# One hybrid encoder layer on one core: elementwise work of the attention stage and of the turn to the channel mixer from GpSimd to VectorE and ScalarE, the turn in two passes, and the down projection's seven products chained in PSUM

## The chip, the core and the metric

The kernel runs on one core of a Trainium2 chip. The metric is the device time of one execution in microseconds; the time before is 1389.1 us, the median of three executions (1386.96 to 1390.07). TensorE (PE) does the matrix products, VectorE (DVE), ScalarE (ACT) and GpSimd (POOL) the elementwise work, and SyncE (SP) issues nearly all transfers.

## The reference, cut to what matters

One encoder layer on 1024 positions of width 1024. A combined input projection feeds gated linear attention (GLA, 4 heads) and differential attention (4 heads, each the difference of two softmax maps); the output projection of both joins the residual; a gated MLP with a depthwise convolution over positions follows, and a last RMSNorm.

```python
h = modulate(rms_norm(x, attn_norm_w), sh_a, sc_a)
q_g, k_g, v_g, r_g, lr_f, lr_b, q_d, k_d, v_d = split_columns(h @ w_in, IN_SIZES)
o_a = rms_norm(gla_forward(q_g, k_g, v_g) + gla_backward(q_g, k_g, v_g), gla_norm_w) * silu(r_g)
p = softmax(q_d @ k_d * scale + bias)            # two maps per head, blocks of 128 queries
o_b = rms_norm((p[0] - lam * p[1]) @ v_d, diff_norm_w) * 0.8
x = x + g_a * (concat(o_a, o_b) @ w_out)
h2 = modulate(rms_norm(x, ffn_norm_w), sh_f, sc_f)
u = conv3(h2 @ w_up)                             # 1024 x 5632
gate, val = split(u, 2)
x = x + g_f * ((silu(gate) * val) @ w_down)      # 2816 x 1024
return rms_norm(x, final_norm_w)
```

Everything is float32, to nearly float32 accuracy.

## The kernel before, in words

**Products.** Each operand of a large product is split into a high part, which ScalarE rounds to the format that TensorE takes (`split`, L369 and L370; `put_hi`, L390), and a low part, the difference, which VectorE or GpSimd takes (L371; `put_lo`, L394). `mm3` (L565 to L567) then runs three matmuls, high by high, low by high and high by low. The up and down projections run as seven products of half-size blocks in place of eight (Strassen's scheme in Winograd's form): sums of blocks are taken on VectorE ahead of a product, sums of results after it.

**Stages in order.** The start and the input projections, in an order written out by hand; from about 355 us the attention stage, in which the GLA heads, the differential attention (32 pairs of a head and a block of queries) and the output projection of the first 512 positions (`gen_wout(0)`) are interleaved; from about 690 us the last of the output projection of the second 512 positions (`gen_wout(1)`); the turn, in which the new x is normalised, transposed and made into the seven operands of the up projection; the up projection, 22 column blocks in pairs (`gen_up`); the down projection (`down_load`, `down_prep`, `down_mms`, `down_out`), and the last norm. Apart from the start the program's order is the order of priority of a list scheduler, which fixes each engine's queue beforehand by its own estimate of times. On the chip each engine takes its queue in order, so an instruction that waits holds all behind it.

**Attention.** `att_probs` makes scores, adds the bias and takes the row maximum on VectorE (L845) and the exponential on ScalarE (L850). `att_T` (L862) transposes the weights on TensorE in two halves, `aT`; one half is copied out by ScalarE (L871), the other by VectorE (L873). `att_out` multiplies by the values (L888) and, after each fourth block, scales by the norm on GpSimd (L898). The GLA heads make `gd` on GpSimd (L1022), and their `norm` (L1093) multiplies by the gate on GpSimd (L1099), rounds on ScalarE and takes the low part on GpSimd.

**The turn.** For each of four i, `gen_wout(1)` transposes two blocks (L380) and evacuates them on VectorE (`b12`, `b22`, L384), forms `t1` = b12 - b11 (L406), `t3` = b22 - b12 (L410), `t2` = t3 + b11 (L411) and `t4` = b21 - t2 (L412), and splits `t1`, `t3` and `b22` with GpSimd's low part, `t2` and `t4` with VectorE's. The first two column blocks of the up projection (`lead` in `strassen`) run beside it, step by step (L1594); the low parts of their weights are GpSimd's (L371).

**The down projection.** The products come in the order p1 p7 p6 p5 p4 p3 p2, each of six steps of up to 24 matmuls, in two sets of four PSUM banks in turn. Each result is taken out of its own bank, and `down_out` forms the sums with VectorE (L1557, L1561, L1562, L1568) and GpSimd (L1558); the gating (`x1_add`, L1538 and L1539) and the last norm's weight (L1565, L1571) are GpSimd's too except in p3 and p2. ScalarE squares the result (`half_sq`, L1545). Loads run three steps ahead (`AHEAD`).

**Buffers.** The pool `big` has 38 tiles of 128x1024, which all stages share; `half` has 5 of 128x512.

## Time and profile before

| | us |
|---|---|
| median of three executions | 1389.1 |
| the profiled execution | 1388.06 |
| its span, first to last instruction | 1386.4 |
| TensorE busy | 1302.7 |
| VectorE busy | 978.6 |
| ScalarE busy | 634.5 |
| GpSimd busy | 389.0 |

The mean granted clock of TensorE is 0.974 of full speed. A busy share is the union of the times of an engine's instructions; matmuls overlap in the records (each lasts 0.39 us and the next starts 0.23 us later), so a busy TensorE is not always one at its peak rate. A number in brackets at the end of a line of the timeline is the idle time of that engine just before the line, and what ended it. In the table of waits the time is summed over all waits of that kind.

### The profile page before, as it was taken

The page shows a single profiled execution, that of the slowest core. Times are in us where ns is not written, and L with a number is a line of the kernel's source. Part 1 is how long each engine was busy: PE and PEld are TensorE (multiplying, and loading weights), DVE is VectorE, ACT ScalarE, POOL GpSimd, SP SyncE. Part 2 cuts the span into 40 slices and gives each one's busy share as a digit, 9 for nine tenths or more (in the row PEclk, how much of TensorE's full clock was granted, in tenths as well). Part 3 has the DMA queues.
Part 4 walks back from the last instruction along what each step waited for, and adds up shares of the span by engine and source line. Part 5 has one row for each costly group of instructions (what it writes and reads, how often), then busy time and mean ns, then how long its engine had stood idle before and what let it go on. Part 6 is the DMA issues. An engine that isn't in the chain of part 4 may idle for free.

```text
span 1386.4 us, 17727 instructions
## 1 busy us (share of the span) xinstructions
PE 1302.7 (94%) x6244; PEld 1069.5 (77%) x6244; DVE 978.6 (71%) x1433; ACT 634.5 (46%) x1058; POOL 389.0 (28%) x284
## 2 busy tenths in 40 slices
...
GB/s 275 216 70 229 175 215 226 297 330 359 343 230 206 210 217 256 284 259 221 207 61 68 130 98 106 100 96 119 129 129 122 114 170 149 388 254 178 143 47 122
DMA packets 197873, 261.57 MB, mean 189 GB/s; under 512 B 13914, under 2 KB 122711, under 8 KB 197783
## 3 DMA queue, kind: packets, MB, share of 16 engines
...
q8 instruction: 49, 0.80, 0.2%
...
q10 hardware_dynamic: 372, 0.04, 0.0%
...
## 4 chain that ended last, share of the span: by engine, by line
PE 69%; DVE 12%; DMA 5%; issue 4%; ACT 3%; POOL 3%; SPq 2%; ACTq 0%; DVEq 0%; POOLq 0%
PE st_up_b L565 4%; PE st_up_b L566 4%; PE st_up_b L567 4%; PE s L842 3%; PE dp L566 3%; PE dp L565 3%; PE dp L567 3%; PE o L888 3%; PE st_up_c L566 3%; PE st_up_c L567 3%; PE st_up_c L565 3%; PE st_up_a L566 2%; PE st_up_a L565 2%; PE st_up_a L567 2%; PE wo_ps L567 2%
## 5 line engine op out<-in xcount | busy, mean ns | idle before, releaser
L371 POOL TENSOR_TENSOR wlo_up<-raw_up,whi_up 128x512 fp32r<-128x512 f32 x132 | 176.3, 1342 | 211.7 <-ACT whi_up L370 203.5
L370 ACT CAST whi_up<-raw_up 128x512 fp32r<-128x512 f32 x132 | 80.8, 618 | 110.9 <-PE st_up_b L566 61.1
L566 PE MATMUL dp<-wlo_dp,dp_hi 128*128 128x512 f32 x308 | 121.1, 393 | 8.3 <-DVE wlo_dp L371 8.3
L565 PE MATMUL dp<-whi_dp,dp_hi 128*128 128x512 f32 x308 | 119.9, 391 | 2.8 <-DVE dacc L1562 2.8
L567 PE MATMUL dp<-whi_dp,db_p 128*128 128x512 f32 x308 | 119.0, 391 | 0.0
L566 PE MATMUL st_up_b<-t_lo,whi_up 128*128 128x512 f32 x264 | 103.4, 392 | 4.4 <-DVE t_lo L394 4.4
L565 PE MATMUL st_up_b<-t_hi,whi_up 128*128 128x512 f32 x264 | 103.6, 393 | 3.8 <-ACT t_hi L390 2.7
L567 PE MATMUL st_up_b<-t_hi,wlo_up 128*128 128x512 f32 x264 | 102.8, 390 | 0.0
L850 ACT ACTIVATE p<-p,mx 128x1024 f32<-128x1024 f32 x64 | 73.5, 1149 | 50.1 <-DVE mx L845 49.8
L845 DVE CUSTOM_DVE_ANT_0 p<-s,bias 128x1024 f32<-128x1024 f32 x64 | 77.3, 1217 | 14.9 <-PE s L842 12.9
L1432 ACT ACTIVATE cv<-u,cw 128x1024 f32<-128x1024 f32 x44 | 53.2, 1210 | 61.0 <-DVE u L433 61.0
L842 PE MATMUL s<-k,q 128*128 128x512 f32 x256 | 78.0, 427 | 2.4 <-DMA k<-k_d 1.5
L566 PEld LDWEIGHTS dp<-wlo_dp,dp_hi 128*128 128x128 f32 x308 | 58.1, 189 | 22.4 <-DVE wlo_dp L371 10.4
L371 DVE TENSOR_TENSOR wlo_dp<-da_p,whi_dp 128x512 fp32r<-128x512 f32 x77 | 67.8, 896 | 8.1 <-ACT whi_dp L370 7.9
L888 PEld LDWEIGHTS o<-vd,aT 128*128 128x128 f32 x512 | 66.7, 199 | 6.8 <-issue 1.7
L371 DVE TENSOR_TENSOR db_p<-db_p,dp_hi 128x1024 fp32r<-128x1024 f32 (+1 forms) x42 | 59.6, 1425 | 16.9 <-ACT dp_hi L370 16.9
L565 PE MATMUL st_up_a<-b_hi,whi_up 128*128 128x512 f32 x176 | 68.9, 392 | 2.3 <-DVE b L384 1.3
L565 PEld LDWEIGHTS dp<-whi_dp,dp_hi 128*128 128x128 f32 x308 | 58.2, 189 | 15.3 <-DVE dacc L1562 3.2
L888 PE MATMUL o<-vd,aT 128*128 128x128 f32 x512 | 68.8, 284 | 0.9 <-ACT aT L871 0.9
L370 ACT CAST whi_dp<-da_p 128x512 fp32r<-128x512 f32 x77 | 46.4, 620 | 49.5 <-PE dp L567 37.5
L566 PE MATMUL st_up_a<-b_lo,whi_up 128*128 128x512 f32 x176 | 68.5, 389 | 0.0
L567 PEld LDWEIGHTS dp<-whi_dp,db_p 128*128 128x128 f32 x308 | 58.3, 189 | 12.1
...
## 6 DMA issues: line engine op xcount, KB each, us to landing
...
```

The costliest lines, as they stand in the source:

```text
L370: S.copy(out=dst_hi, in_=src)
L371: lo_eng.tensor_tensor(out=dst_lo, in0=src, in1=dst_hi.bitcast(F32), op=ALU.subtract)
L565: T.matmul(ps, wh, rh, start=first, stop=False, skip_group_check=more)
L566: T.matmul(ps, wh, rl, start=False, stop=False, skip_group_check=more)
L567: T.matmul(ps, wl, rh, start=False, stop=last, skip_group_check=more)
L842: T.matmul(s[:, tsl(n)], q4[:, 2 * m + sw, :], kd[h][m][:, tsl(n)], start=(sw == 0), stop=(sw == 1))
L845: V.tensor_tensor_reduce(out=t, in0=s, in1=bias, scale=1.0, scalar=3.0e38, op0=ALU.add, op1=ALU.min, accum_out=mx)
L850: S.activation(t, t, AF.Exp, scale=-1.0, bias=mx, accum_out=z[:, m:m + 1])
L888: T.matmul(o_ps, aT[:, k, :], vd[h // 2][k // 4][:, k % 4, psl(h % 2)], start=(k == 0), stop=(k == KT - 1))
L1432: S.activation(t, u[b], AF.Identity, scale=cw[:, 44 + ci:45 + ci], bias=cw[:, 132 + ci:133 + ci])
```

## The change

What it does:

- The turn leaves `gen_wout` and becomes `gen_turn`, and a string (`'turn'`) gives the order in which its steps (T, U, u), the steps of the first two column blocks (a letter and 0 or 1) and the rest of the output projection (L, W) are put into the program. A first pass (four T) makes `t1`, `b22` and `t3`, a second (two U, then u) `t2`, then the low parts of `t3` and `t4`. All low parts of the turn are VectorE's; the evacuation of `b22` becomes ScalarE's (`'tb'`). `t3` is kept in pairs of `big` in place of `half`.
- The first two column blocks take their products in the order 1 2 5 3 6 7 4, products 1 and 2, 5 and 3, and 6, 7 and 4 each chained in one bank; the low parts of all their weights are VectorE's (`'lv'`).
- Attention: both halves of `aT` are copied by ScalarE (`'aTs'`); `gd` (`'q3v'`), the scaling of `on` (`'onv'`), and the gate and the low part in GLA's `norm` (`'goe'`) become VectorE's. The list of output projection steps in each attention block (`'wo'`) is shifted.
- The down products come in the order p1 p2 p6 p7 p5 p4 p3. p2 adds to p1's bank, p7 and p4 to p6's, p3 to p5's, so that sums of results are formed in PSUM. GpSimd's `dacc` sums go; p2 gates on VectorE and adds on GpSimd; p4's last norm is one VectorE instruction of 128x1024 in place of the weight on GpSimd. `a12` is loaded twice, and the x of the first four tiles comes at step 3 in place of 27, that of the others at 21 in place of 22.

```diff
-    KN = {... 'wo': [3, 2, 2, 2, 2, 2, 1, 1, 2, 4, 3, 3, 3, 2, 3, 3], ... 'x01': (3, 4), ...}
+    KN = {... 'wo': [3, 2, 2, 2, 2, 2, 2, 2, 2, 3, 3, 3, 3, 2, 3, 3], ... 'x01': (3, 3), ...
+          'dord': 'p1 p2 p6 p7 p5 p4 p3', 'aTs': '01', 'ons': 0, 'goe': 'VV', 'q3v': 1, 'onv': 1,
+          'turn': 'L p0 p1 W a0 a1 b0 b1 T T T T s0 s1 U U c0 c1 d0 d1 u', 'tb': 1,
+          'los': {'t1': 'VVVV', 'b22': 'VVVV', 't2': 'VVVV', 't3': 'VVVV', 't4': 'VVVV'}, 'lv': '1253674'}
...
-            return w_block(src, f"{name}{n}", G)
+            return w_block(src, f"{name}{n}", V if lead and str(n) in KN["lv"] else G)
...
+        if lead:
+            s1 = half(f"s1_{name}", F32, [P, TH], "sum")
+            c1 = half(f"c1_{name}", F32, [P, 4, P])
+            w, w2 = block(a11, 1), block(a12, 2)
+            add(c1, a21, a22)
+            sub(a21, a11, a21)
+            sub(a11, c1, a11)
+            sub(a12, a12, a11)
+            yield
+            A = mm_ps(f"st_{name}a")
+            into(A, w, "b11", True)
+            S.copy(out=s1, in_=A)
+            yield
+            into(A, w2, "b21", False)
+            out(0, 0, A, None)
+            yield
+            w = block(c1, 5)
+            yield
+            C = s_ps(f"st_{name}c")[:, tsl(0)]
+            into(C, w, "t1", True)
+            out(1, 1, C, s1)
+            yield
+            into(C, block(a12, 3), "b22", False)
+            out(0, 1, C, s1)
+            yield
+            Bk = mm_ps(f"st_{name}b")
+            into(Bk, block(a11, 6), "t2", True)
+            out(0, 1, Bk, dst(0, 1))
+            yield
+            into(Bk, block(a21, 7), "t3", False)
+            out(1, 1, Bk, dst(1, 1))
+            yield
+            into(Bk, block(a22, 4), "t4", False)
+            out(1, 0, Bk, s1)
...
-            if g == KN["aT"]:
+            if str(g) in KN["aTs"]:
...
-        G.tensor_tensor(out=on, in0=on, in1=ss.unsqueeze(2).to_broadcast([P, 4, P]), op=ALU.mult)
+            V.tensor_tensor(out=on, in0=on, in1=ss.unsqueeze(2).to_broadcast([P, 4, P]), op=ALU.mult)
...
-            G.tensor_tensor(out=o, in0=o, in1=r_t[:, tsl(th)], op=ALU.mult)
+            eg[KN["goe"][0]].tensor_tensor(out=o, in0=o, in1=r_t[:, tsl(th)], op=ALU.mult)
...
-            split(hi, lo, o, G)
+            split(hi, lo, o, eg[KN["goe"][1]])
...
+        for i in range(KT // 2):
+            if i % 2 == 0:
+                t3p[i // 2] = big(f"b12_{i}", F32, PAIR)
+            b12, b22, t1 = t3p[i // 2][:, i % 2, :], half(f"b22_{i}"), half(f"t1_{i}")
+            f32_block(xn_late, i, a_ff, sh_ff, b12, "h2n", "ao")
+            f32_block(xn_late, i + 4, a_ff, sh_ff, b22, "h2n", "ao", KN["tb"])
+            V.tensor_tensor(out=t1, in0=b12, in1=h2f[i // 2][:, i % 2, :], op=ALU.subtract)
+            put_hi(h2b, "t1", i, t1)
+            put_hi(h2b, "b22", i, b22)
+            V.tensor_tensor(out=b12, in0=b22, in1=b12, op=ALU.subtract)
+            put_lo(h2b, "t1", i, t1, eng("t1", i))
+            put_lo(h2b, "b22", i, b22, eng("b22", i))
+            yield
+        part = lambda i: [p[:, i % 2, :] for p in (t3p[i // 2], h2f[i // 2], h2f[2 + i // 2])]
+        for i in range(KT // 2):
+            t3, b11, b21 = part(i)
+            V.tensor_tensor(out=b11, in0=t3, in1=b11, op=ALU.add)
+            put_hi(h2b, "t2", i, b11)
+            V.tensor_tensor(out=b21, in0=b21, in1=b11, op=ALU.subtract)
+            put_lo(h2b, "t2", i, b11, eng("t2", i))
+            if i % 2:
+                yield
+        for n, k in (("t3", 0), ("t4", 2)):
+            for i in range(KT // 2):
+                put_of(n, i, part(i)[k])
...
+    LOADS = {"p1": ("a11",), "p2": ("a12", "a21"), "p6": ("a22",), "p7": (), "p5": ("a21", "a22"), "p4": (), "p3": ("a12",)}
+    BANK = {"p1": ("A", True), "p2": ("A", False), "p6": ("B", True), "p7": ("B", False), "p4": ("B", False),
+            "p5": ("C", True), "p3": ("C", False)}
...
+            mm3(ps_of[t], bh[:, i, psl(t)], bl[:, i, psl(t)], *ws[i], new and u == 0, u == NU - 1, not new)
...
+        elif p == "p2":
+            x1_add(t, 0, ps, half(f"dt_{p}{t}"), (V, G))
+            half_sq(t, 0)
+        elif p == "p6":
+            tmp = half(f"dt_{p}{t}", tag="sum")
+            V.tensor_tensor(out=tmp, in0=ps, in1=s1, op=ALU.add)
+            s2_of[t] = tmp
         elif p == "p7":
+            V.tensor_tensor(out=kept(s3_of), in0=ps, in1=s1, op=ALU.add)
         elif p == "p5":
-            tmp = half(f"dt_{p}{t}")
-            V.tensor_tensor(out=tmp, in0=ps, in1=acc2[t], op=ALU.add)
-            V.tensor_tensor(out=acc1[t], in0=ps, in1=acc1[t], op=ALU.add)
+            tmp = s3_of[t // 2][:, t % 2, :]
+            V.tensor_tensor(out=tmp, in0=ps, in1=tmp, op=ALU.add)
             x1_add(4 + t, 1, tmp, tmp, (G, G))
             half_sq(4 + t, 1)
             G.tensor_tensor(out=x1[4 + t][:, TH:], in0=x1[4 + t][:, TH:], in1=fin_w[:, TH:], op=ALU.mult)
-            x1_add(4 + t, 0, acc1[t], acc1[t], (G, G))
+            x1_add(4 + t, 0, s2_of[t], s2_of[t], (G, G))
         elif p == "p4":
-            V.tensor_tensor(out=acc2[t], in0=ps, in1=acc2[t], op=ALU.add)
-            x1_add(t, 1, acc2[t], acc2[t], (G, G))
+            tmp = half(f"dt_{p}{t}")
+            V.tensor_tensor(out=tmp, in0=ps, in1=s1, op=ALU.add)
+            x1_add(t, 1, tmp, tmp, (G, G))
             half_sq(t, 1)
-            G.tensor_tensor(out=x1[t][:, TH:], in0=x1[t][:, TH:], in1=fin_w[:, TH:], op=ALU.mult)
-            p1 = p1_of[t // 2][:, t % 2, :]
-            x1_add(t, 0, p1, p1, (G, G))
+            finish(t, False)
...
+            V.scalar_tensor_tensor(out=o, in0=o, scalar=rs, in1=fin_w, op0=ALU.mult, op1=ALU.mult)
+            nc.sync.dma_start(out=out[0, psl(t), :], in_=o)
```

## Rows read from the trace of the kernel before

**Rows 1.** The first part of the page: busy us of each engine, its share of the span, and its instructions.

```profile
PE 1302.7 (94%) x6244; PEld 1069.5 (77%) x6244; DVE 978.6 (71%) x1433; ACT 634.5 (46%) x1058; POOL 389.0 (28%) x284
```

**Rows 2.** The view by windows of 20 us, some of them: the window, its length, busy us (and instructions) of PE, PEld, DVE, ACT and POOL, then the granted clock, the share of DMA and GB/s.

```profile
380.00:400.00 20.00, 17.71 (x105) 15.68 (x104) 14.96 (x31) 12.85 (x26) 1.89 (x1) 0.83 0.91 238
...
420.00:440.00 20.00, 15.77 (x91) 13.36 (x91) 11.18 (x19) 12.34 (x24) 5.92 (x6) 0.83 0.77 211
...
500.00:520.00 20.00, 18.51 (x118) 15.07 (x116) 12.28 (x21) 9.35 (x20) 3.67 (x3) 0.91 1.02 319
...
720.00:740.00 20.00, 11.45 (x36) 7.16 (x37) 19.93 (x19) 9.49 (x18) 14.70 (x10) 0.70 0.11 32
...
1200.00:1220.00 20.00, 20.00 (x90) 16.57 (x89) 19.14 (x22) 11.02 (x16) 0.00 (x0) 1.00 1.05 386
...
1320.00:1340.00 20.00, 16.07 (x69) 12.33 (x67) 18.17 (x13) 9.99 (x20) 20.00 (x11) 1.00 0.12 40
1340.00:1360.00 20.00, 18.96 (x76) 15.51 (x77) 15.73 (x26) 10.57 (x25) 2.13 (x2) 0.91 0.14 56
```

**Rows 3.** The same view with windows for whole stages: the turn, a part of the up projection, the down projection, the attention stage.

```profile
704.20:760.00 55.80, 41.77 (x169) 30.39 (x168) 46.63 (x53) 24.00 (x46) 34.04 (x23) 0.88 0.21 66
860.00:1080.00 220.00, 220.00 (x978) 182.31 (x977) 181.96 (x235) 98.02 (x137) 106.76 (x81) 1.00 0.39 118
1153.90:1378.00 224.10, 213.00 (x926) 173.99 (x924) 179.54 (x190) 100.86 (x169) 79.52 (x44) 0.99 0.52 184
...
355.00:690.00 335.00, 315.25 (x1948) 270.68 (x1947) 230.83 (x424) 170.50 (x353) 46.22 (x38) 0.96 0.80 241
```

**Rows 4.** The timeline of TensorE near the end, two matmuls 40 starts apart.

```profile
1355.03 0.39 PE L566 MATMUL dp<-wlo_dp,dp_hi 128*128 128x512 f32 x1
...
1364.10 0.39 PE L567 MATMUL dp<-whi_dp,db_p 128*128 128x512 f32 x1
```

**Rows 5.** VectorE's groups in the turn (704.2 to 748 us), by line and form: busy us, mean ns of one.

```profile
L394 DVE TENSOR_TENSOR t_lo<-h2f,t_hi 128x512 fp32r<-128x512 f32 x8 | 8.8, 1126 | 0.0
L384 DVE TENSOR_SCALAR b<-h_ps,a_ff,modc 128x512 f32<-128x512 f32 x8 | 6.2, 800 | 0.0
...
L1330 DVE TENSOR_SCALAR x<-x,rs_f 128x1024 f32<-128x1024 f32 x4 | 3.3, 838 | 3.1 <-ACT rs_f L366 3.1
L406 DVE TENSOR_TENSOR t<-b,h2f 128x512 f32<-128x512 f32 x4 | 2.7, 678 | 0.0
```

**Rows 6.** The timeline of VectorE and of GpSimd in the turn, and of SP's queue at its end.

```profile
720.84 1.77 DVE L412 TENSOR_TENSOR h2f<-h2f,h2f 128x512 f32<-128x512 f32 x1
...
720.33 1.74 POOL L394 TENSOR_TENSOR t_lo<-t,t_hi 128x512 fp32r<-128x512 f32 x1
...
737.12 29.25 SPq L1413 DMA_DIRECT2D raw_up<-in_w_up_dram  x11
```

**Rows 7.** GpSimd's groups in the attention stage (330 to 690 us), and the copies of `aT` in it (355 to 690 us) by VectorE and by ScalarE.

```profile
L371 POOL TENSOR_TENSOR go<-go,ohi 128x512 fp32r<-128x512 f32 x8 | 10.7, 1339 | 6.0 <-ACT ohi L370 5.3 <-DVE mx L845 0.7
L1099 POOL TENSOR_TENSOR go<-go,gr 128x512 f32<-128x512 f32 x8 | 10.2, 1276 | 62.0 <-DVE go L1098 56.6 <-PE aT_ps L869 5.4
...
L898 POOL TENSOR_TENSOR on<-on,oss 128x512 f32<-128x512 f32 x8 | 9.9, 1236 | 180.7 <-ACT oss L897 144.3 <-DVE mx L845 36.3
L1022 POOL TENSOR_TENSOR gd<-gq,dc_sh 128x1024 f32<-128x1024 f32 x4 | 7.6, 1906 | 36.5 <-DMA k_d<-qk_hi 21.9 <-DMA gq<-g_d 14.6
...
L873 DVE COPY aT<-aT_ps 128x512 f32<-128x512 f32 x32 | 22.0, 687 | 7.9 <-PE aT_ps L869 7.7
...
L871 ACT COPY aT<-aT_ps 128x512 f32<-128x512 f32 x32 | 18.6, 583 | 19.9 <-PE aT_ps L869 19.7
```

**Rows 8.** The timeline at two stops of TensorE in the attention stage: at 382 us (VectorE, TensorE) and at 431 us (ScalarE, TensorE), and TensorE at the two stops that follow.

```profile
380.34 1.70 DVE L1049 SCALAR_TENSOR_TENSOR gs<-gs,dc_sc,gs 128x128 f32<-128x128 f32 x1
...
382.36 0.65 PE L869 MATMUL aT_ps<-ident,p 128*128 128x128 f32 x4 [2.29 <-DVE on L889]
...
429.84 0.62 ACT L370 CAST ohi<-go 128x512 fp32r<-128x512 f32 x1 [2.17 <-POOL go L1099]
...
431.00 3.06 PE L1034 MATMUL u_ps<-gv,kn 64*128 64x128 f32 x16 [3.83 <-ACT kn L1029]
...
468.54 3.06 PE L1034 MATMUL u_ps<-gv,kn 64*128 64x128 f32 x16 [4.32 <-ACT kn L1029]
...
516.08 1.77 PE L842 MATMUL s<-k,q 128*128 128x512 f32 x4 [1.49 <-DMA k<-k_d]
```

**Rows 9.** VectorE's groups in the down projection, from 1160 to 1240 us and from 1276 to 1316 us.

```profile
L371 DVE TENSOR_TENSOR wlo_dp<-da_p,whi_dp 128x512 fp32r<-128x512 f32 x31 | 20.8, 684 | 4.2 <-ACT whi_dp L370 4.0
L371 DVE TENSOR_TENSOR db_p<-db_p,dp_hi 128x1024 fp32r<-128x1024 f32 x17 | 20.5, 1218 | 6.1 <-ACT dp_hi L370 6.1
...
L371 DVE TENSOR_TENSOR wlo_dp<-da_p,whi_dp 128x512 fp32r<-128x512 f32 x10 | 14.4, 1444 | 0.0
L371 DVE TENSOR_TENSOR db_p<-db_p,dp_hi 128x1024 fp32r<-128x1024 f32 x5 | 10.1, 2017 | 0.0
```

**Rows 10.** GpSimd's costliest group in the down projection (1236 to 1386 us); and what TensorE waited for over the whole run, two lines: us in total, times, longest.

```profile
L1538 POOL TENSOR_TENSOR dacc<-dacc,g_f 128x512 f32<-128x512 f32 x8 | 16.0, 2014 | 4.9 <-DVE dacc L1568 4.9
...
PE dp L566 <- DVE wlo_dp L371: 8.3, 5, 2.4
...
PE dp L565 <- DVE dacc L1562: 2.8, 1, 2.8
```

167 lines of the change are left out of this document (84 added, 83 removed).

## The prediction

> **What bounds the kernel now.** I read the busy shares first, then the windows, then the waits of the stages in which TensorE is not full. TensorE is busy for 1302.7 of 1386.4 us [rows 1], so nothing but TensorE's stops, and stretches at its lower clock level, can be won. In the up projection there are none: 220.00 of 220.00 us busy at a granted clock of 1.00, while VectorE has 182 of 220 [rows 3]. TensorE's rate at full clock is one 128x512 matmul per 0.227 us, from two matmuls 40 starts and 9.07 us apart [rows 4]. By that rate three stages lose time. The turn: 169 instructions in 55.8 us, of which 32 are transposes; 137 x 0.227 = 31.1 us, the transposes 6 us at most, so at least 18.7 us are lost [rows 3]. The down projection: 7 x 11 x 4 x 3 = 924 matmuls are 209.7 us in a stretch of 224.1, 14.4 lost [rows 3]. Attention: 335.0 - 315.3 = 19.7 us idle, and a mean clock of 0.96, some 13 us more [rows 3].
>
> One cause runs through all three. A VectorE instruction with two operands in SBUF takes 0.68 us where GpSimd is quiet and 1.77 where GpSimd works beside it [rows 5, 6]; in the down projection the same low parts go from 684 to 1444 ns and from 1218 to 2017 ns once GpSimd is loaded [rows 9]. In the turn VectorE is full (19.93 of 20 us) with such stretched instructions, TensorE has 11.45 of 20 and the clock falls to 0.70 in that window, after TensorE's stops [rows 2].
>
> **The turn: -12 us (-17 to -2).** GpSimd leaves it: its 19 low parts go to VectorE at 0.68 us each (the row of L406; 1.77 if GpSimd were still at work). VectorE's new work: first pass 4 x (0.80 for b12 + 4 x 0.68) = 14.1; second pass 12 x 0.68 = 8.2; low parts of t3 and t4 8 x 0.68 = 5.4; low parts of the weights of products 5 3 6 7 4 for two columns 6.8; ten result sums 6.8: together 41.3 us [rows 5]. The sums and weights of products 1 and 2 (12 x 0.68 = 8.2) come ahead of the last output projection part, and VectorE has room there. TensorE's work in the same stretch is 168 x 0.227 = 38.1 plus the transposes, 44.1. Counted from the last output projection matmul, VectorE can begin after the norm of x: 3.1 us idle and 3.3 of scaling in the rows of before, 6.4 [rows 5]; products 1 and 2 of both columns (48 matmuls, 10.9 us) cover that, and the chained order puts t1 and b22, which come first, under the next products. The first pass and two weights end at 6.4 + 15.5 = 21.9, the second, with two more weights, at about 31.5; TensorE is through with a, b, c, d and the transposes at 10.9 + 6 + 10.9 = 27.8: a stop of some 4 us. The last low part is done near 45, and 3 to 5 us of matmuls follow: 48 to 50 against 44.1. With the hand-overs to ScalarE I take a loss of 7 in place of 18.7: -12. The good end is a loss of 2 (-17). The bad end: if VectorE gets nothing back from the quiet GpSimd, it has 19 x 0.68 - 4 x 0.80 = 9.7 us more to do, which puts the loss at 17 (-2). One thing has no row: t3 in `big` tiles and the second pass hold more of the 38 tiles, so the loads for the third column, which SP's queue issues from 737.12 on, over 29 us [rows 6], start later against their use; I count that in the 7, up to 5 us.
>
> **Attention: -7 us (-17 to +5).** GpSimd gives up 38.4 us [rows 7]: `gd` 4 x 1.91, `on` 8 x 1.24, the gate and the low part 8 x 1.28 and 8 x 1.34. VectorE takes them at 4 x 1.22 (the 1218 ns row, [rows 9]) + 24 x 0.68 = 21.2 and hands 32 copies of 0.687 to ScalarE, 22.0: even. ScalarE gets 32 x 0.583 = 18.7 on 170.5 of 335, 56% [rows 3, 7]. What is won sits at the stops. At 380 us a 128x128 step that should be short took 1.70 beside `gd`, and TensorE stood for 2.29 behind VectorE [rows 8]: -2, and the stretch at half clock that follows (0.83 of 20 us, 3.4 us, [rows 2]): -3.4. At 431 and 468 ScalarE waits for GpSimd's gate (2.17), the copy `kn` stands behind it, and TensorE waits 3.83 and 4.32 [rows 8]; the gate on VectorE is 0.6 shorter, so -1.3 for both, because the chain of norm, gate, rounding and copy stays. At 516 a load is late behind a store of the low part [rows 8]: -1. Sum -7.7; +0.7 for the second half of `aT`, which now comes up to 0.58 later. Good end: all four stops (11.9) and 5 us of clock, -17. Bad end: a quarter of the 32 second halves uncovered, 4.7, and nothing won. The shifted list of output projection steps moves work within a stage that TensorE bounds; I cost it at nothing, with 2 us either way inside these ends.
>
> **The down projection: -4 us (-7 to +4).** After p5 and p4 GpSimd runs 40 instructions of some 1.95 us now (8 of them the group at 2014 ns, [rows 10]); after the change p5 keeps 20, p4 keeps 8, and p2 has 4. So the stretch after p5, where TensorE waits for `dacc` 2.8 us and part of the 8.3 for `wlo_dp` [rows 10], stays; that after p4 (1320 to 1346, TensorE 16.07 of 20, then clock 0.91, [rows 2]) loses 12 x 1.95 = 23 us of GpSimd beside VectorE. Of its 3.9 idle and 1.8 of clock I count two thirds: -4. Chaining adds waits: p2's first matmul into a bank waits for ScalarE's copy of p1 out of it, p7's and p4's for VectorE's sums. Behind those stand only the next matmuls, and a bank is asked for again three banks (2 us) later than its result is done, so they are free unless VectorE is late; 4 x 0.68 = 2.7 at worst. The second load of `a12` is 6 x 0.5 MB = 3.1 MB, 8 us at the 386 GB/s that the full queues give there [rows 2], with 4 MB of x now partly in the same stretch. SP issues them behind each other, ahead of the operands of the next steps; the lookahead of three steps (16 us) covers it, and if it does not, half of the 8 us shows: the +4.
>
> **Sum.** 1388.1 - 12 - 7 - 4 = 1365 for the profiled execution (its span of 1386.4 and 1.7 around it); the median, 1389.1, is 1 us above it. A difference under 0.2% (2.8 us) could not be told from no change.
>
> **The rivals.**
> As forecast, between 1352 and 1377: chance 0.58.
> VectorE becomes the bound. It is full in the turn already [rows 2], and gets 9.7 us more; if the end of GpSimd's work returns little of the stretching, the turn wins 2, attention, where its load is even, 3, the down projection 3: 1380 (1377 to 1385). For it: the full window; against it: 1.77 beside 0.68 in the same turn [rows 5, 6]. Chance 0.18. The Trainium skill bears on this one: its page "Perfetto Trace Analysis", under Optimizing Scalar/DVE Operations, advises to offload from a saturated VectorE to ScalarE or even GpSimd, the reverse of this edit, though it adds that the two share a read port, so that it might not help. By the first half the time would be the 1380 above, by the second the 1365; the rows named here speak for the second.
> The stops go with their half-clock stretches too, attention -17, turn -17, down -7: 1347. For it: each half-clock window in attention has a stop before or in it [rows 2, 8]; against it: the GLA chain stays long. Chance 0.13.
> The schedule made beforehand shifts and stops move elsewhere, so that nothing is won: 1388. Chance 0.04.
> Slower: ScalarE's queue in attention. Each block's second half of `aT` stands behind the first there; if TensorE has less than 0.58 us of other work between transposes and values, all 32 cost 18.7, and VectorE's low parts wait for ScalarE's rounding where GpSimd waited (5.3, [rows 7]), ahead of the row maxima: +24, against -16 from the other stages: 1396. It decides once those gaps are uncovered in over two thirds of the blocks. Against it: ScalarE is at 56%, and its copies wait 19.9 us for TensorE, not TensorE for them [rows 7]. Chance 0.07.
>
> **How the numbers follow.** Likeliest 1365. The range leaves out the slower and the unchanged case and half of the largest gain: 1347 to 1384. Faster 0.58 + 0.18 + 0.13 = 0.89, same 0.04, slower 0.07.
>
> **What would show it.** GpSimd with nothing between the last `on` and the third column, VectorE's instructions of the turn at 0.68 throughout, the clock at 1.00 there, and the turn's 169 instructions in about 44 us. In attention the low part of `go` on VectorE and stops at `kn` of 3 us or more still. In the down projection stops behind p5 but few after p4. Wrong would be: TensorE waiting for ScalarE's `aT`, stops on loads at 1190 to 1215, or a stop of many us at the third column.

## The result, and the profile after

The changed kernel takes 1372.3 us (median of 7 executions, 1368.7 to 1380.7) beside 1389.1 for the kernel before (7 executions on the same chip): a ratio of 0.9877, 95% interval 0.9854 to 0.9900. The forecast was 1365, between 1347 and 1384. The profiled execution took 1372.34 us, its span 1370.6; the span of before was 1386.4, so the two traces differ by 15.8 us. The busy line of the page after, against [rows 1]:

```profile
PE 1296.4 (95%) x6244; PEld 1065.0 (78%) x6244; DVE 957.6 (70%) x1447; ACT 649.3 (47%) x1086; POOL 287.5 (21%) x218
```

GpSimd gave up 101.5 us. VectorE, which took most of those instructions and handed 22 us of copies to ScalarE, is busy for 21 us less: its instructions got shorter. The windows of whole stages, columns as in [rows 3]: attention from the first transpose of the weights to the last matmul of the output projection, the turn, the same part of the up projection as before, the down projection.

```profile
363.68:702.08 338.40, 319.92 (x1956) 273.17 (x1955) 231.80 (x430) 189.73 (x390) 10.51 (x11) 0.95 0.77 233
702.20:760.00 57.80, 49.56 (x209) 37.85 (x208) 43.72 (x73) 28.49 (x55) 7.83 (x5) 0.94 0.23 73
860.00:1080.00 220.00, 220.00 (x978) 182.33 (x977) 182.77 (x232) 99.48 (x139) 105.69 (x80) 1.00 0.37 108
1146.40:1361.50 215.10, 211.09 (x925) 172.77 (x924) 165.79 (x185) 96.76 (x160) 55.69 (x32) 1.00 0.58 204
```

Each is read as before: what TensorE's matmuls would take at 0.227 us each is taken from the length. The turn: 209 instructions, 32 of them transposes (6 us): 177 x 0.227 + 6 = 46.2, a loss of 11.6 in place of 18.7 (the kernel before, over 57.80 us from 704.20, comes to 18.7 too). The down projection: 209.7 of 215.1, a loss of 5.4 in place of 14.4. The up projection's full part is unchanged. Where TensorE still stops, from its timeline:

```profile
424.14 1.73 PE L1051 MATMUL u_ps<-gv,kn 64*128 64x128 f32 x16 [1.43 <-ACT kn L1046]
...
461.43 3.09 PE L1051 MATMUL u_ps<-gv,kn 64*128 64x128 f32 x16 [3.65 <-ACT kn L1046]
...
509.69 1.17 PE L853 MATMUL s<-k,q 128*128 128x512 f32 x4 [2.28 <-DMA k<-k_d]
...
618.45 0.69 PE L380 MATMUL h_ps<-ident,x 128*128 128x128 f32 x2 [2.67 <-DVE x L1350]
...
745.90 0.47 PE L576 MATMUL st_up_b<-t_hi,whi_up 128*128 128x512 f32 x1 [2.12 <-DVE u L418]
...
802.66 0.50 PE L576 MATMUL st_up_a<-b_hi,whi_up 128*128 128x512 f32 x1 [2.90 <-DVE u L418]
...
1239.62 0.47 PE L576 MATMUL dp<-whi_dp,dp_hi 128*128 128x512 f32 x1 [2.52 <-DVE dt_p L1620]
```

Of [rows 8], the stop at 382 is gone, but two of 1.00 and 0.57 us stand before score matmuls at 384.82 and 386.99; those at `kn` are 1.43 and 3.65 in place of 3.83 and 4.32, and TensorE waits longer for the load of `k` (2.28 for 1.49). Three stops stand at a chained bank or a sum of results on VectorE: 745.90, 802.66 and 1239.62. Of the down projection's waits in [rows 10] only 0.7 us for `wlo_dp` is left.

In the turn VectorE's two-operand instructions, against [rows 5, 6] (its groups from 702.2 to 746 us, mean ns behind the busy time):

```profile
L371 DVE TENSOR_TENSOR wlo_up<-raw_up,whi_up 128x512 fp32r<-128x512 f32 x8 | 5.5, 699 | 3.1 <-PE h2n_ps L380 2.3 <-ACT whi_up L370 0.8
L394 DVE TENSOR_TENSOR t_lo<-h2f,t_hi 128x512 fp32r<-128x512 f32 x8 | 5.4, 702 | 0.0
...
L1382 DVE TENSOR_TENSOR t<-b,h2f 128x512 f32<-128x512 f32 x4 | 2.7, 686 | 0.0
```

From 720 to 740 us VectorE is full as before, but with 36 instructions in place of 19 [rows 2], and TensorE is busy for 16.09 us in place of 11.45, at a granted clock of 0.93 in place of 0.70:

```profile
720.00:740.00 20.00, 16.09 (x61) 11.07 (x60) 20.00 (x36) 11.49 (x21) 0.00 (x0) 0.93 0.05 14
```

Between the traces the last matmul of the output projection moved by 2.0 us (704.1 to 702.1; 1.3 of them lie ahead of the attention stage), the turn and the up projection shortened by 5.5 (449.9 to 444.4), and the down projection, first to last matmul, by 8.9 (223.7 to 214.8). The forecast was 7, 12 and 4.

### The profile page after: what moved, and what is told of

It is laid out like the page before. It is cut to its first block, busy times and chain, and to the rows that moved or that the text cites. A ratio compares the mean times of both kernels' runs of the same rounds, so it can differ in the third digit from the quotient of the medians.

```text
span 1370.6 us, 17665 instructions
## 1 busy us (share of the span) xinstructions
PE 1296.4 (95%) x6244; PEld 1065.0 (78%) x6244; DVE 957.6 (70%) x1447; ACT 649.3 (47%) x1086; POOL 287.5 (21%) x218
## 4 chain that ended last, share of the span: by engine, by line
PE 72%; DVE 11%; DMA 9%; issue 3%; ACT 2%; SPq 1%; POOL 1%; ACTq 0%; DVEq 0%; POOLq 0%
PE st_up_b L576 4%; PE st_up_b L577 4%; PE st_up_b L578 4%; PE s L853 3%; PE dp L576 3%; PE dp L577 3%; PE o L899 3%; PE dp L578 3%; PE st_up_a L576 3%; PE st_up_a L578 3%; PE st_up_a L577 3%; PE st_up_c L577 2%; PE st_up_c L578 2%; PE st_up_c L576 2%; PE pr_qk L576 2%
## 5 line engine op out<-in xcount | busy, mean ns | idle before, releaser
L371 POOL TENSOR_TENSOR wlo_up<-raw_up,whi_up 128x512 fp32r<-128x512 f32 x120 | 162.3, 1358 | 309.9 <-ACT whi_up L370 188.2
L578 PE MATMUL dp<-whi_dp,db_p 128*128 128x512 f32 x308 | 115.6, 389 | 0.0
L371 DVE TENSOR_TENSOR wlo_dp<-da_p,whi_dp 128x512 fp32r<-128x512 f32 x77 | 61.7, 823 | 20.3 <-ACT whi_dp L370 20.2
L576 PEld LDWEIGHTS dp<-whi_dp,dp_hi 128*128 128x128 f32 x308 | 57.8, 188 | 16.9 <-issue 2.9
L577 PEld LDWEIGHTS dp<-wlo_dp,dp_hi 128*128 128x128 f32 x308 | 57.8, 188 | 13.3 <-DVE wlo_dp L371 1.6
L578 PE MATMUL st_up_a<-b_hi,wlo_up 128*128 128x512 f32 x176 | 67.3, 390 | 0.0
L578 PEld LDWEIGHTS dp<-whi_dp,db_p 128*128 128x128 f32 x308 | 57.8, 188 | 11.9
```

The source lines that it names most:

```text
L371: lo_eng.tensor_tensor(out=dst_lo, in0=src, in1=dst_hi.bitcast(F32), op=ALU.subtract)
L576: T.matmul(ps, wh, rh, start=first, stop=False, skip_group_check=more)
L577: T.matmul(ps, wh, rl, start=False, stop=False, skip_group_check=more)
L578: T.matmul(ps, wl, rh, start=False, stop=last, skip_group_check=more)
```

## The experiments

The theory after the result had three parts. Theory 1: GpSimd was worth little in attention, because the stops at `kn` are made by the order of the queues. Theory 2: in the turn GpSimd's contention was what cost, and what is left is VectorE handing over results late. Theory 3: the down projection won so much because eight GpSimd instructions left the crowded stretch behind p5. Ratios are to the kernel before on the same chip; "us" is the ratio times 1389.1. The last three columns are lengths in one trace of each, from start to start: first `aT_ps` to last `wo_ps` matmul, from there to the first `dp`, first to last `dp`. "Span x clock" is the span times the mean granted clock, on the mean of a kernel's executions (before: the 71 beside the experiments): the span less what TensorE's lower clock level costs, if TensorE had work all that time. Its standard errors are 0.4 to 1.4.

| run | ratio (95%) | us | span x clock | attention | turn and up | down |
|---|---|---|---|---|---|---|
| before | 1 | 1389.1 | 1350.3 | 339.1 | 449.9 | 223.7 |
| changed | 0.9877 (0.9854, 0.9900) | 1372.0 | 1340.7 | 338.4 | 444.4 | 214.8 |
| changed, again | 0.9898 (0.9865, 0.9931) | 1374.9 | 1343.2 | 335.8 | 447.8 | 214.3 |
| attention as before | 0.9922 (0.9895, 0.9949) | 1378.3 | 1343.3 | 337.8 | 446.7 | 216.7 |
| down as before | 0.9930 (0.9909, 0.9951) | 1379.4 | 1346.8 | 337.8 | 442.8 | 221.6 |
| turn's low parts on GpSimd | 0.9942 (0.9921, 0.9963) | 1381.0 | 1344.9 | 334.5 | 450.1 | 215.6 |
| `kn` on VectorE | 0.9905 (0.9883, 0.9928) | 1375.9 | 1342.3 | 331.6 | 442.8 | 215.0 |
| `kn` ahead of the norm | 0.9923 (0.9895, 0.9951) | 1378.4 | 1342.8 | 332.3 | 442.8 | 216.5 |
| p5's gating held | 0.9963 (0.9942, 0.9984) | 1384.0 | 1346.3 | 336.0 | 444.3 | 225.7 |
| `aT` split | 0.9962 (0.9936, 0.9987) | 1383.8 | 1348.1 | 347.4 | 445.4 | 216.7 |
| attention's moves undone | 0.9944 (0.9926, 0.9963) | 1381.3 | 1347.8 | 342.8 | 444.9 | 214.2 |
| `gd` and `on` on GpSimd | 0.9906 (0.9878, 0.9933) | 1376.0 | 1345.5 | 336.3 | 442.2 | 215.6 |
| weights of 7 and 4 on GpSimd | 0.9867 (0.9844, 0.9890) | 1370.6 | 1341.8 | 336.6 | 444.2 | 213.8 |
| product 6 ahead of 3 | 0.9855 (0.9818, 0.9892) | 1369.0 | 1338.0 | 336.5 | 441.9 | 215.8 |

Executions of one kernel spread by about 0.5% to either side, so two ratios tell a difference apart only from some 0.4%. The trace of a stage tells more, but it spreads too: in the kernels whose edit does not touch it, attention lies between 334.5 and 338.4, turn and up between 442.2 and 447.8, down between 213.8 and 216.7.

**The changed kernel once more.**

> The changed kernel once more, unedited, on the chip and beside the same runs of the kernel before as the three edits that go with it. If the differences between executions are those of TensorE's clock alone (seven executions lie between 1368.7 us at a mean granted clock of 0.979 and 1380.7 at 0.972), span times mean clock is 1340 to 1342 us here too, the median is 1371 to 1376, and a second trace has the same stops at the same instructions (1.4 and 3.7 us at kn, 2.1 at the third chained bank of the turn, 2.5 at p7 in the down projection), with half-clock stretches in other places of the attention stage. If stops move as well, span times clock differs by more than 2 us.

A median of 1374.0 us, ratio 0.9898. The stops that were named stand at the same instructions with the same lengths: 1.43 and 3.65 at `kn`, 2.12 in the turn, 2.90 in the up projection, 2.53 at p7. Others differ: there is one of 1.06 us for the load of `q` at 432.60, and attention's idle time is 20.2 us for 18.5. The clock did not follow the stops alike; windows of 10 us, the granted clock is the third column from the end, first this kernel's first trace, then the second:

```profile
420.00:430.00 10.00, 7.91 (x44) 6.47 (x43) 6.63 (x11) 6.59 (x16) 0.00 (x0) 0.79 0.90 250
430.00:440.00 10.00, 10.00 (x71) 8.94 (x71) 7.81 (x15) 8.05 (x17) 0.20 (x1) 0.87 0.76 261
```

```profile
420.00:430.00 10.00, 7.91 (x58) 6.62 (x57) 6.94 (x12) 6.62 (x15) 0.00 (x0) 1.00 0.89 258
430.00:440.00 10.00, 8.88 (x69) 7.41 (x68) 7.92 (x15) 9.09 (x19) 0.20 (x1) 1.00 0.88 286
```

TensorE is busy for the same 7.91 us with the same stop of 1.43, once partly at the lower level, with 44 instructions, and once at full clock, with 58. The turn in the second trace, from the last output projection matmul, loses 57.8 - (184 x 0.227 + 6) = 10.0 us:

```profile
700.60:758.40 57.80, 50.53 (x216) 38.52 (x215) 45.20 (x74) 29.96 (x57) 8.26 (x6) 0.94 0.23 73
```

Span times mean clock is 1340.7 us on the mean of the first 7 executions (standard error 1.0) and 1343.2 of these 6 (1.4). So the expectation of 1340 to 1342 was missed by 1 us, and the two differ by the 2 us and more that I had named as a sign of stops that move, though hardly beyond these errors. I use span times clock below where a median says too little; the kernel before has 1349.9 to 1351.0.

**Attention alone put back.**

```diff
-    'wo': [3, 2, 2, 2, 2, 2, 2, 2, 2, 3, ...], 'aTs': '01', 'goe': 'VV', 'q3v': 1, 'onv': 1
+    'wo': [3, 2, 2, 2, 2, 2, 1, 1, 2, 4, ...], 'aTs': '0', 'goe': 'GG', 'q3v': 0, 'onv': 0
```

> The changed kernel with the attention stage alone put back as it was: one half of aT copied by VectorE, gd, the scaling of on, the gate and the low part in norm on GpSimd, and the old list of output projection steps. Theory 1 (the stops at kn come from ScalarE's own queue, in which the copy kn stands behind a rounding that waits for norm and gate; taking GpSimd out of it shortens that chain by about 1 us only): +2 us on 1372 (0 to +4), the last matmul of the output projection at 703 to 706 us in place of 702.1, stops of TensorE at kn of 3.5 to 4.5 us. Rival 1 (the predicted 7 us were won, and were lost again in the same stage through ScalarE's 32 more copies): also about +2, so this run sizes the part, and the run with the copies alone put back decides. Rival 2 (the attention stage owes its 2 us to nothing in these edits, only to the trace): 0, the last matmul at 702.

1378.3 us, 5 above the changed kernel (1373.5, the mean of its two rows), hardly told apart from it; by span times clock 1.4 us more (1343.3, against 1341.9 over the 13 executions of the changed kernel). The stage in the trace is 337.8, as the changed kernel's; the last matmul came at 702.06, not at the 703 to 706 that theory 1 expected. Its stops are those of [rows 8] again: 1.99, 3.84, 4.33 and 1.86 us. So attention brought some 1 to 5 us, hardly clear of the noise, and what by which edit this run can't say.

**`aT` split; all moves undone; two of them undone.** Three edits of the same four settings:

```diff
-    'aTs': '01'
+    'aTs': '0'
```

> The changed kernel with one edit in attention: the second half of aT is copied by VectorE again (32 copies of 0.69 us), ScalarE keeps the first. Theory 1 (GpSimd's work was worth little in attention, and ScalarE has room for the copies): 0, between -1 and +2 us, the stage unchanged within 2 us and only the wait for aT of 1.2 us at 626 us gone. Rival 1 (the moves off GpSimd won up to the 7 us forecast, and ScalarE's 32 more copies gave them back): -3 to -6 us, waits for ScalarE in the stage shorter. Rival 2 (VectorE is the tighter engine there): +3 and more, waits of TensorE for VectorE's row maxima or on.

```diff
-    'goe': 'VV', 'q3v': 1, 'onv': 1
+    'goe': 'GG', 'q3v': 0, 'onv': 0
```

> The changed kernel with ScalarE keeping both halves of aT and the old moves undone: gd, the scaling of on, the gate and the low part in norm go back to GpSimd, so that VectorE is rid of 21 us of work on both counts. After the run with half of aT put back on VectorE (6 to 8 us slower) there are two readings. Theory A (VectorE's load is what counts in attention; 22 us of copies were worth 6 to 8 us, so 21 us of other work are worth about as much): -3 to -7 us against the changed kernel's 1372 to 1374, VectorE busy about 207 us of the stage in place of 228. Theory B (GpSimd's slowness costs as much: its work stretches VectorE's beside it, and the gate on the norm chain takes 1.3 us in place of 0.69): 0 to +4, the stops at kn back at 3.8 and 4.3 us, as in the kernel before.

```diff
-    'q3v': 1, 'onv': 1
+    'q3v': 0, 'onv': 0
```

> The changed kernel with only gd and the scaling of on back on GpSimd (12 instructions, 10.5 us on VectorE); the gate and the low part of norm, which lie on the chain ahead of kn, stay on VectorE. Theory A (VectorE's load counts): -2 to -4 us, the stops at kn as in the changed kernel (1.4 and 3.7). Theory B (GpSimd stretches VectorE's work beside it): +1 to +3, with the 2 us stop of TensorE behind on at 382 us back, where gd runs beside the state's scan.

With the copies back on VectorE 1383.8 us, 10 slower; with the moves undone 1381.3, 8 slower; with `gd` and `on` alone on GpSimd 1376.0, not told apart by the ratio. The attention windows of the three, in this order:

```profile
369.09:716.51 347.42, 319.97 (x1956) 272.00 (x1955) 248.62 (x462) 172.29 (x358) 10.51 (x11) 0.95 0.75 227
```

```profile
369.73:712.54 342.81, 315.88 (x1956) 269.18 (x1955) 215.46 (x402) 189.77 (x390) 48.46 (x38) 0.97 0.76 230
```

```profile
364.10:700.36 336.26, 313.77 (x1957) 266.74 (x1956) 227.46 (x418) 188.92 (x390) 25.43 (x22) 0.97 0.76 235
```

TensorE idles for 27.5, 26.9 and 22.5 us (length less busy), against 18.5 and 20.2 in the two traces of the changed kernel. For `aT` split rival 2 holds by its price: VectorE, with 248.6 us of work for 231.8, is the tighter engine. The longest waits are not the ones that it named, though: 3.39 us for the load of `k`, 4.24 for the x that VectorE scales for the turn's first half. For the moves undone theory B holds in its sign, at twice its price: VectorE has 16 us less to do, and it is slower all the same. The stop at the second `kn` is 4.33 again, and at the end of the stage TensorE waits for GpSimd and for what comes behind it:

```profile
700.00 0.66 PE L924 MATMUL oT_ps<-ident,on 128*128 128x128 f32 x4 [1.21 <-POOL on L915]
701.44 0.50 PE L576 MATMUL wo_ps<-whi_wo,ok 128*128 128x512 f32 x1 [0.78 <-ACT ok L934]
```

These two, 1.45 us for VectorE at 696, 3.50 at 624 (2.67 in the changed kernel) and 1.7 more at `kn` make up most of what is lost. Putting back both halves (with the old list of steps) costs less than either alone: moves and copies are a swap, and each half needs the other. The third run splits the moves: `gd` and `on`, 4 instructions of 1.9 us and 8 of 1.2 on GpSimd [rows 7], make no difference that the ratio can tell, but by span times clock they cost 3.6 us (standard error 1.2) of the 5.9 that all moves cost, with 2 us and more of idle time beyond the changed kernel's. The 2 us stop behind `on` that theory B expected at 382 is not there (0.56 and 0.77 for `aT` are, at 383 and 385). The other 2 us, hardly told apart, are left for the gate and the low part, which stand ahead of `kn`: in this run the stops there are 0.90 and 3.65, with both back on GpSimd 2.48 and 4.33.

**The copy `kn` on VectorE, and ahead of the norm.**

```diff
-            S.copy(out=kn, in_=kps)
+            V.tensor_copy(out=kn, in_=kps)
```

> The changed kernel with one edit: the copy kn of the GLA heads (eight of them) out of PSUM is VectorE's in place of ScalarE's. Theory 1 (kn stands in ScalarE's queue behind a rounding that waits for the norm chain): the stops of TensorE at kn (1.43, 3.65 us) go or fall under 1 us, with part of the half-clock stretch behind each, total -3 to -7 us on 1372. Rival 1 (VectorE's queue holds kn as long, behind the row maxima and the gate): the stops stay at 1.5 to 4 us with VectorE as the engine named, total -1 to +2. Rival 2 (what stops there is TensorE's own order, the transposes of kn coming too late for a copy of 0.6 us to be hidden): the stops stay at 1.4 and more whoever copies, total 0.

```diff
             S.copy(out=kn, in_=kps)
+            if later:
+                later.pop()()
...
-        norm(1, *n1)
+        if h < 2:
+            later.append(lambda: norm(1, *n1))
+        else:
+            norm(1, *n1)
```

> The changed kernel with the second norm of GLA heads 0 and 1 put into the program behind the next head's first copy kn, so that kn no longer stands behind the norm chain in any queue; engines and work are the same. Theory 1 (the stops at kn are a matter of queue order: kn's transposes are done by 417.9 and 457.8 us, the copy is issued at 423.5 and 460.8, behind a rounding that waits for the gate): the two stops go from 1.4 and 3.7 to under 1.5 us together, total -2 to -6 us on 1372 with the half-clock stretches behind them. Rival (the delay comes back at the next reader: the norm's late low parts hold TensorE's output projection or the five half tiles): stops of 2 us and more at another instruction within 30 us, total -1 to +3.

1375.9 and 1378.4 us: neither is faster than the changed kernel, by span times clock either (1342.3 and 1342.8 for 1341.9). On VectorE the copy stands behind the same chain (timeline of TensorE, then of VectorE at 423 us):

```profile
425.45 1.68 PE L1051 MATMUL u_ps<-gv,kn 64*128 64x128 f32 x16 [2.29 <-ACT ohi L370]
...
460.88 1.82 PE L1051 MATMUL u_ps<-gv,kn 64*128 64x128 f32 x16 [3.16 <-ACT ohi L370]
```

```profile
423.27 0.75 DVE L1115 SCALAR_TENSOR_TENSOR go<-go,cols,gsq 128x512 f32<-128x512 f32 x1 [1.36 <-ACT gsq L1114]
424.06 0.69 DVE L1117 TENSOR_TENSOR go<-go,gr 128x512 f32<-128x512 f32 x1
424.67 0.68 DVE L1046 COPY kn<-kn_ps 128x512 f32<-128x512 f32 x1
```

`kn`'s transposes were through at 422.3; VectorE held the copy behind the norm and the gate until 424.67. The profile names ScalarE's rounding, but the copy's end, 425.35, lies 0.1 us before the matmul. That is rival 1. Put ahead of the norm, `kn` keeps TensorE for 0.39 us at most, but other stops of the same size are there in its place:

```profile
456.63 1.80 PE L853 MATMUL s<-k,q 128*128 128x512 f32 x4 [2.58 <-issue]
...
492.94 1.13 PE L1114 MATMUL ms<-gsq,inv_dv 128*128 128x512 f32 x2 [1.33 <-ACT gsq L1109]
```

TensorE's idle time in attention is 18.6 and 18.4 us in these two (331.64 less 313.00 busy, 332.34 less 313.98), inside the 17.9 to 20.3 of the seven traces that leave attention alone. Their stages are 4 us shorter in the trace because TensorE had a higher granted clock in that execution: 0.983 over the span, where the mean over all executions of the two is 0.979 and 0.976. So theory 1 is half right: the stops are a matter of queue order, but taking them away doesn't shorten the stage.

**The turn's low parts on GpSimd.**

```diff
-    'los': {'t1': 'VVVV', 'b22': 'VVVV', ..., 't3': 'VVVV', ...}, 'lv': '1253674'
+    'los': {'t1': 'GGGG', 'b22': 'GGGG', ..., 't3': 'GGGG', ...}, 'lv': ''
```

> The changed kernel in which the turn keeps its two passes and its order of products, but the low parts of t1, b22 and t3 and those of the first two columns' weights go back to GpSimd, as in the kernel before. Theory 2 (GpSimd's work beside VectorE is what stretches VectorE's instructions, 1.77 beside 0.68 us): VectorE's additions in the turn at 1.1 us and more on the mean in place of 0.70, the turn's loss 16 to 19 us in place of 11.7, total +4 to +8 us on 1372. Rival (the order in two passes brought the 5.5 us, and VectorE is now the longest queue of the turn): VectorE gets rid of some 26 x 0.7 = 18 us of work, the wait of 2.1 us at 745.9 us goes, total 0 to -4 us.

1381.0 us, 7 to 8 slower (3.0 by span times clock; the mean granted clock is 0.975 for 0.978), and turn and up at 450.1, where the kernel before has 449.9: theory 2, though the loss in the turn, 15.9 below, is a hair under its 16 to 19. The order in two passes, which this run keeps, brings nothing over these stages by itself that can be told. VectorE's groups in the turn, and the stop at the chained bank:

```profile
L394 DVE TENSOR_TENSOR t_lo<-h2f,t_hi 128x512 fp32r<-128x512 f32 x6 | 7.8, 1307 | 0.0
L1382 DVE TENSOR_TENSOR t<-b,h2f 128x512 f32<-128x512 f32 x4 | 5.3, 1344 | 0.0
...
L384 DVE TENSOR_SCALAR b<-h2n_ps,a_ff,modc 128x512 f32<-128x512 f32 x4 | 3.2, 805 | 5.3 <-PE h2n_ps L380 5.3
```

```profile
748.69 0.69 PE L576 MATMUL st_up_b<-t_hi,whi_up 128*128 128x512 f32 x1 [4.21 <-DVE u L418]
```

The window of the turn, from the last output projection matmul:

```profile
700.60:758.40 57.80, 47.22 (x190) 36.19 (x189) 45.46 (x49) 26.66 (x52) 39.03 (x26) 0.88 0.20 64
```

VectorE has 49 instructions there in place of 73, and is busy for 45.5 us in place of 43.7; the loss is 57.8 - (158 x 0.227 + 6) = 15.9. The addition of L1382 takes 1344 ns for 686. The evacuation of L384, which reads PSUM, takes 805 ns here and 808 in the changed kernel. The Trainium skill says as much on its page "SBUF — State Buffer", under Who interferes with whom: a VectorE instruction with two inputs in SBUF contends with a GpSimd instruction that reads SBUF, and one with at most one SBUF input, outside the modes that take both ports, does not. These rows agree.

**The weights of products 7 and 4 on GpSimd.**

```diff
-    'lv': '1253674'
+    'lv': '12536'
```

> The changed kernel with one edit in the turn: the low parts of the weights of products 7 and 4 of the first two column blocks (four of 0.7 us on VectorE) go to GpSimd, which is idle there. Theory 2 (anything on GpSimd beside VectorE costs VectorE more than it takes from it: with twelve low parts and all weights there, the stage was 5.7 us longer): 0 to +3 us, the wait for the result sum at the third chained bank 2 us or more. Rival (VectorE is the longest queue of the turn's end, and four instructions less in it bring the sum of product 6 forward by 1.3 us): -1 to -3 us, that wait under 1.2 us.

1370.6 us, turn and up 444.2: no difference that can be told. The wait stayed, at 2.44 us, with VectorE's queue ahead of it (timeline of GpSimd, then of VectorE):

```profile
737.06 6.45 POOL L371 TENSOR_TENSOR wlo_up<-raw_up,whi_up 128x512 fp32r<-128x512 f32 x3 [4.06 <-ACT whi_up L370]
```

```profile
739.51 2.87 DVE L394 TENSOR_TENSOR t_lo<-h2f,t_hi 128x512 fp32r<-128x512 f32 x2
742.30 0.68 DVE L418 TENSOR_TENSOR u<-st_up_c,s_up__7324 128x512 f32<-128x512 f32 x1
742.90 0.68 DVE L418 TENSOR_TENSOR u<-st_up_b,u 128x512 f32<-128x512 f32 x1
```

Two low parts take 2.87 us beside GpSimd, where two take 1.3 without it: what VectorE was spared it paid in length. In the 57.80 us from 700.40 it is busy for 46.5 us with 71 instructions; in the two traces of the changed kernel for 43.7 with 73 and 45.2 with 74.

**Product 6 ahead of product 3.** In the changed kernel VectorE's queue ahead of the stop at 745.90 was this:

```profile
742.04 0.71 DVE L418 TENSOR_TENSOR u<-st_up_c,s_up__7308 128x512 f32<-128x512 f32 x1
742.64 0.70 DVE L394 TENSOR_TENSOR t_lo<-h2f,t_hi 128x512 fp32r<-128x512 f32 x1
743.24 1.31 DVE L371 TENSOR_TENSOR wlo_up<-raw_up,whi_up 128x512 fp32r<-128x512 f32 x2
744.44 0.71 DVE L418 TENSOR_TENSOR u<-st_up_c,s_up__7324 128x512 f32<-128x512 f32 x1
745.04 0.71 DVE L418 TENSOR_TENSOR u<-st_up_b,u 128x512 f32<-128x512 f32 x1
```

Product 7 adds to the bank of product 6, so it waits until the sum of 745.04 has read it; that sum waits for product 3's, to which it adds.

```diff
-            into(C, block(a12, 3), "b22", False)
-            out(0, 1, C, s1)
-            yield
             Bk = mm_ps(f"st_{name}b")
             into(Bk, block(a11, 6), "t2", True)
-            out(0, 1, Bk, dst(0, 1))
+            out(0, 1, Bk, s1)
             yield
+            into(C, block(a12, 3), "b22", False)
+            out(0, 1, C, dst(0, 1))
+            yield
```

> The changed kernel with one edit in the turn: in the first two column blocks product 6 comes ahead of product 3 in the program, and its result is added to s1 at once, product 3's being added to that; the number of operations is the same. In the changed kernel product 6 of a column is through at about 738 us, but its sum waits on VectorE for product 3's sum and for low parts until 745.0, and product 7, chained in the same bank, starts at 745.9 after a stop of 2.1 us. Theory 2 (the loss at the turn's end is this hand-over of a chained bank, by order and not by VectorE's load): the stop falls under 0.5 us, one half-clock stretch (1.7 us) may go with it, total -2 to -4 us on 1372 to 1374, turn and up projection 440 to 443 us in place of 444.4 and 447.5. Rival (VectorE is full there, so that the wait only goes to the next operand, the low parts of t3 or t4, or t2 is late for product 6): a stop of 1.5 to 3 us at another instruction of the turn, total -1 to +2.

1369.0 us, the lowest ratio of all (0.9855), though its interval covers the changed kernel's; span times clock is 1338.0 (standard error 0.7) against 1340.7 and 1343.2. Turn and up 441.9. Product 6's sums now come at 737.77 and 738.97, and the stop is 0.52 (timeline of TensorE, of VectorE, and the window of the turn from the last output projection matmul):

```profile
746.91 0.47 PE L576 MATMUL st_up_b<-t_hi,whi_up 128*128 128x512 f32 x1 [0.52 <-DVE u L418]
```

```profile
737.77 0.68 DVE L418 TENSOR_TENSOR u<-st_up_b,s_up__7308 128x512 f32<-128x512 f32 x1
...
738.97 0.68 DVE L418 TENSOR_TENSOR u<-st_up_b,s_up__7324 128x512 f32<-128x512 f32 x1
```

```profile
701.00:758.80 57.80, 51.96 (x229) 40.46 (x228) 49.94 (x78) 31.30 (x59) 10.53 (x8) 0.97 0.23 72
```

229 instructions in the same 57.80 us: 197 x 0.227 + 6 = 50.7, a loss of 7.1 in place of 11.6. The kernel gives VectorE the same instructions; their order was at fault. One part of this kernel's gain is not the edit's own: the stop of 2.90 at 802.66 is 0.53 here, with one of 1.24 at 812.78, and so or nearly so it is in five other kernels, those with the weights of 7 and 4 or the turn's low parts on GpSimd among them.

**The down projection put back.** The diff is that of the change, reversed, in the down projection alone (`down_prep`, `down_mms`, `down_out` and the place of the x loads).

> The changed kernel with the down projection alone put back: order p1 p7 p6 p5 p4 p3 p2, each product in its own bank, sums on VectorE and GpSimd, the weight on GpSimd. Theory (the part's gain is its own: fewer and earlier GpSimd instructions behind p5 and p4): +9 us on 1372 (+7 to +11), the down stage 223 to 225 us in place of 214.8 from its first to its last matmul, stops of TensorE after p5 and p4 of 2 to 3 us each. Rival (the stage was helped by what comes before it, a quieter end of the up projection or earlier loads): +2 to +5, the down stage at 217 to 220.

1379.4 us, 6 slower, the stage at 221.6 us: below the 223 to 225 expected, above the rival's 217 to 220. The stops come back where they were in [rows 10], after p5 and p4: 2.31 us for `dacc` at 1290.9 and 2.14 for `wlo_dp` at 1331.1, with 0.9, 0.9 and 0.7 between them. The part's gain is its own, 5 to 7 us in this pair.

**p5's gating held.**

```diff
-            x1_add(4 + t, 0, s2_of[t], s2_of[t], (G, G))
+            x1_add(4 + t, 0, s2_of[t], tmp, (G, G))
```

> The changed kernel with one edit in the down projection: p5's gating of the first half writes its product into the tile that the second half's gating still reads, so that these eight GpSimd instructions come after p5's second-half work (as in the kernel before) and not right after p6. Theory 3 (the down projection won more than forecast because these eight left the crowded stretch after p5): GpSimd has 20 instructions at 1290 to 1330 us, VectorE's low parts there take 1.4 us and more, stops of 1 to 3 us come back after p5, total +2 to +5 us on 1372. Rival (the gain came from sums formed in PSUM, fewer GpSimd instructions in all and none behind p4): 0 to +1, the down stage 214.5 to 216 us.

1384.0 us, 10 to 11 slower, the stage at 225.7 us, longer than in the kernel before. The first of the eight on GpSimd in the changed kernel and, below it, the first of them here; then TensorE's longest stop here; then the windows 1320 to 1340 of the changed kernel and of this one:

```profile
1236.15 2.17 POOL L1597 TENSOR_TENSOR dt_p<-dt_p,g_f 128x512 f32<-128x512 f32 x1 [21.38 <-DVE dt_p L1620]
```

```profile
1314.01 1.74 POOL L1597 TENSOR_TENSOR dp<-dt_p,g_f 128x512 f32<-128x512 f32 x1
```

```profile
1342.04 0.79 PE L577 MATMUL dp<-wlo_dp,dp_hi 128*128 128x512 f32 x1 [5.67 <-DVE wlo_dp L371]
```

```profile
1320.00:1340.00 20.00, 19.32 (x85) 15.36 (x84) 16.02 (x20) 10.38 (x21) 5.55 (x4) 1.00 0.11 35
```

```profile
1320.00:1340.00 20.00, 13.09 (x56) 9.95 (x54) 20.00 (x11) 6.41 (x11) 20.00 (x11) 0.93 0.34 124
```

The same instructions on the same engines, eight of them 78 us later and more, and TensorE has 13.09 of 20 us in place of 19.32. Over the stage it idles for 10.8 us in place of 4.0, and the granted clock is 0.97 in place of 1.00. Theory 3 is shown, at more than twice the price that I expected of it (4.4 us by span times clock, the rest being clock). The run does not size the part that the eight have in the 8.4 us won: held back, they meet other instructions than in the kernel before. What lets the eight go early is in the change: p6's sum `s2` is final at p6, while before `acc1` was still added to at p5.

## Why the prediction was right, and where its terms were off

**The cause.** "One cause runs through all three" held in the turn and in the down projection; in attention no run parts it from the places of the instructions in their queues. VectorE's two-operand instructions went to 686 to 702 ns in the turn once GpSimd was quiet. The trace of before shows it instruction by instruction: of its 128x512 ones with both operands in SBUF from 704 to 760 us, the 12 beside which GpSimd did nothing took 676 to 693 ns, the 8 that GpSimd's work overlapped for over nine tenths of their time 1135 to 1775, 1686 on the mean (from 1160 to 1380 us, 70 of 684 ns and 19 of 1571 on the mean); six of the turn's with an operand in PSUM took 682 to 692, overlapped or not. And of the experiments that put GpSimd's work beside VectorE's, the turn's low parts cost 7 to 8 us and p5's gating 10 to 11, and the weights of 7 and 4 gave back in length what they took in number. The rival in which VectorE becomes the bound fell by its price: VectorE is full from 720 to 740 still, but with GpSimd idle it does more in less time (73 instructions in 43.7 us of the turn's 57.80; before, 56 in 48.6). Of the Trainium skill's page "Perfetto Trace Analysis", under Optimizing Scalar/DVE Operations, the runs bear out the advice for ScalarE and the reservation on GpSimd: `aT`'s copies back on VectorE cost 10 us, and for instructions with both operands in SBUF the way back to GpSimd cost time too (450.1 for 444.4 us in the turn and the up projection).

**The turn: -12 forecast, some -5.5 measured** (449.9 against a mean of 444.4 over ten traces of kernels that leave it alone). The loss went from 18.7 to 11.6 and 10.0 (the second trace: 216 instructions from 700.60 to 758.40), not to 7. The term too small was the hand-over: I counted instructions on VectorE and a stop of some 4 us between the passes, and wrote of no wait for a sum into a chained bank here, though I did so for the down projection. The bank of products 6 and 7 cost 2.1 us and, it seems, a stretch at the lower clock level; in the one trace without that stop the loss is 7.1, the value forecast. The rest was lost further on, in the up projection's first columns: at 802.66 TensorE waits 2.90 us for a sum of results that stands in VectorE's queue. I had put that price down to late loads, and no stop on a load is there. Of the signs, "the clock at 1.00" was wrong (0.93 from 720 to 740), and the 169 instructions took 49.0 and 47.4 us, not 44; with product 6 ahead of 3 they take 43.5.

**Attention: -7 forecast, some -2.6 measured** (339.1 against a mean of 336.5 over the seven traces that leave it alone; by the run with the stage put back -5 with 5 either way, 1.4 by span times clock, and 337.8 in its trace, so that the size is not shown clear of the spread). The stops on which the term rested moved by more than their share: -2.3 at 382, -2.4 and -0.7 at `kn`. What failed is the step that took each stop by itself: idle time taken away at one instruction came back at another (1.00 and 0.57 before score matmuls at 385 and 387, `k` 2.28 for 1.49, x 2.67 for 1.35 on VectorE, 1.2 for `aT`), as in the two runs on `kn`. The stage's idle time went from 21.1 us to 18.5 and 20.2 in the two traces, and the clock did not improve: 0.95 and 0.96 after, 0.96 before. The balance "even" for VectorE was right, and more binding than I wrote: half of the swap alone costs 8 to 10 us. The slower rival, ScalarE's queue, fell: TensorE waited 1.2 us for `aT`, once.

**The down projection: -4 forecast, -8.4 measured** (223.7 against a mean of 215.3 over the eleven traces that leave the part alone, -7 to -10). I wrote that "the stretch after p5 ... stays", since p5 keeps 20 GpSimd instructions. It keeps 12: eight of them hang on p6's sum alone and were scheduled there. I had followed the instructions by the product whose code holds them, not by the value that they wait for. What the sums formed in PSUM brought by themselves no run shows; with the eight held back the stage is no shorter than before (225.7 for 223.7). The bound from the chained banks was right (2.5 us at p7, 2.7 at worst forecast), and the loads cost nothing.

**The sum.** 2.6 + 5.5 + 8.4 is 16.5, against 17.1 and 14.2 by the two ratios: right in sign and range, with one term half of what it should be and two of them twice too large or more. That the total is off by 7 us only is in part luck: the turn and attention brought 11 less than forecast, the down projection 4 more. By span times clock the change is worth 8.4 us (1350.3 to 1341.9); the rest is a mean granted clock of 0.978 in place of 0.973, which the prediction had in some of its terms (3.4 us in attention, two thirds of 1.8 in the down projection) and not as a part of its own. The bound of 0.2% under which "a difference ... could not be told from no change" was too fine: it is some 0.4% for two kernels.

**Left open.** The stop of 2.6 us before a score matmul, in the run with `kn` ahead, has no cause that the profile names, and no run shows how much of attention's remaining 18 to 20 us of idle time can be had at all. The version with product 6 ahead of 3 has the lowest time of all measured; that it beats the changed kernel is shown by the turn's rows, in one trace, and by span times clock (1338.0 for 1341.9), not by the median.
